# Attention of a hybrid encoder step: three engines in one written order, units in three lags, and prompt masks written by VectorE

## The chip, the cores and the metric

The kernel runs on one core of one Trainium2 chip. Its time is device microseconds from the start to the end of the program. The core has a matrix engine (TensorE, PE), three engines for elementwise work (VectorE or DVE, ScalarE or ACT, GpSimd or POOL), a sync engine (SP) that issues most transfers, and DMA queues. Each engine works through its own instructions one after another, and semaphores hold an instruction back until what it reads has been written and what it overwrites has been read.

## The reference

One inference step of an encoder with two layers, in float32, on 384 tokens: 256 frames of one prompt and 16 frames of each of 8 running sequences. Layer 0 mixes with a Mamba block, layer 1 with attention; behind each stands a PEER layer (a product-key mixture of 16384 experts). Only the attention is touched here. Cut to it:

```python
kv = rmsnorm(h, norm_kv) @ a_w_kv + a_b_kv            # 1024 -> 512: four heads of K and V, 64 wide
q = xn @ a_w_q[j] + a_b_q[j]                          # 1024 -> 1024: 16 heads, four to each K/V head
# prompt: a frame sees the keys of its own chunk of 64 and of the two chunks before it
probs = sink_softmax(jnp.where(valid, scores, -jnp.inf), sinks)   # the sink is one more logit, without a value
# sequence: the 128 cached keys and the 16 new ones
mix = o @ a_w_o[j] + a_b_o[j]
h = h + mix
h = h + peer(rmsnorm(h, norm_ffn[l]), ...)
```

## The kernel before, in words

The program is mamba, peer, attention, peer. Tokens lie in three blocks of 128: blocks 0 and 1 are the prompt, block 2 the eight sequences. Every large product is made exact enough by splitting both operands: a weight tile `raw` (128x1024) arrives by a DMA of SP (L152), ACT casts it to `hi` (L132), and DVE writes the rest to `lo` (L133). A product is then three matmuls: hi by hi, hi by lo, lo by hi. The helper `split` does it; `ring` gives the two `hi` and two `lo` buffers, a third where a pool for it is named (then `hix` and `lox`).

**Head.** The scaled rows of h are turned by PE (L897) and split into `khi`, `klo` and `qhi`, `qlo`; the K/V projection accumulates over eight row tiles in `accs` (L183). Then come query tiles 0 and 1 (`q_tile`: 24 matmuls at L168 to L170, ACT adds the bias into `qT` at L936, DVE copies the sequences' part to `qs` at L939), and K is turned to `kT` (L954, L956).

**Units.** 16 units of work follow, in the list `todo`. A prompt unit (p) is one block of queries and one K/V head: block 0 has 128 keys (called p0 below), block 1 has 256 (p1). A sequence unit (s) is two sequences and two K/V heads, 256 keys. The order is p0, p1, p0, p1, s, s, s, s, and that again, with two K/V heads to each half. A unit passes through these steps:

- scores: PE lays a mask (a matmul of a bf16 mask by the identity `idb`, L978) into the unit's PSUM banks and adds the score products (L988 or L998). A p unit has two banks, an s unit one.
- DVE takes the largest score (L1005, one reduction to a bank) and from it the negative offset `nm` (L1006) and the sink's exponent `es` (L1007).
- ACT takes the exponents to `sm`, two to a bank, each with its row sum in `den` (L1014), and that of `es` (L1008).
- DVE makes the shares: sum, reciprocal, and `sm` scaled (L1017, L1018, L1021).
- PE turns `sm` (L1031); ACT copies the first bank of a p unit to `pT` (L1037), DVE the other bank and that of an s unit (L1035).
- PE takes the products with the values (L1049 or L1062), ACT copies them to `oT` (L1051, L1066).

**Order.** In the loop (L1089 to L1106) a turn i writes the scores of unit i, the transposes of unit i-2 and the values of unit i-3. `pin` keeps PE's matmuls in the order in which they are written. For DVE and ACT nothing is fixed: the tile scheduler orders their instructions. Six query tiles (`q_at`) and four output terms (the last four turns) lie between the units. An output term is one 128-row tile of w_o against the split `oT` (`ohi`, `olo`): 12 matmuls for the two prompt blocks, 6 for the third block.

**Tail.** After the loop come the third block's first four terms (their weights loaded a second time), then terms 4, 5 and the pair 6 and 7 for all blocks. The adds of the result to h (`add`, L1122), the squares for the norm (L205) and the first projection (L1227) belong to the second call of `peer`. So does the load of its first weight tile `p_w_q`, which ACT casts to `hix`.

The masks come from POOL, which fills three bf16 tiles (L866 to L874) before it issues the seven loads of constants (L849 to L856).

Of the kernel before, what the change touches and what calls it, by code (L numbers as in the profile page):

```python
# [19 lines left out]
P = 128  # L20
# [48 lines left out]
def encoder_step(ctx: ExitStack, tc: tile.TileContext, t_in, t_out):  # L69
# [759 lines left out]
    def attention():  # L829
        with ExitStack() as c:  # L830
# [30 lines left out]
            mask0 = T(one, [P, 2, P], BF16, tag="mask0")  # L861
            mask1 = T(one, [P, 2, NP], BF16, tag="mask1")
            maskS = T(one, [P, NSEQ, NP], BF16, tag="maskS")

            def masked():
                pool.memset(mask0, 0.0)  # L866
                pool.memset(mask0[0:64, :, 64:128], NEG)
                pool.memset(mask1, 0.0)
                pool.memset(mask1[0:64, :, 192:256], NEG)
                pool.memset(mask1[64:128, :, 0:64], NEG)  # L870
# [18 lines left out]
            kw = {0: load_raw(t_in["w_kv"][0:P, :], 512)}  # L889
            turned = {}  # L890
# [8 lines left out]
            with in_order():  # L899
# [3 lines left out]
                hi0 = ring(512, F32R, "hi", 2)  # L903
                lo0 = ring(512, F32R, "lo", 2)
                act.copy(hi0, kw[0])
# [3 lines left out]
                dve.tensor_tensor(lo0, kw[0], hi0.bitcast(F32), op=OP.subtract)  # L909
                nrm.scale(1, xn[:, 1], 2)  # L910
                for b, n in ((2, 3), (0, 2), (1, 1)):
# [3 lines left out]
                accs = [[bank([P, 512])] for _ in range(NB)]  # L915
                for k in range(KD):
# [9 lines left out]
                split(qhi[:, KD - 1], qlo[:, KD - 1], turned[KD - 1], scale=gcol[:, 1, KD - 1:KD])  # L926
                dve.tensor_copy(idb, ident)
            with tc.issue_after(nrm.last.ins):
                masked()
                constants()  # L930
            kctx.__exit__(None, None, None)

            def q_tile(ct):
                ps = bank([P, NT])
                gemm_cols(ps, load_split(t_in["w_q"][ct]), qhi, qlo, 0, NT)
                act.activation(qT[:, ct], ps, AF.Identity, bias=bq[:, ct:ct + 1])  # L936
                n, g2 = divmod(ct, 2)
                for half in range(2):
                    dve.tensor_copy(qs[:, :, n, 2 * g2 + half],  # L939
                                    qT[64 * half:64 * half + 64, ct, NP:].rearrange("p (s t) -> p s t", t=TS))  # L940

            q_tile(0)
            q_tile(1)
            for b in range(NB):
                dve.tensor_tensor(kv[:, b], accs[b][0], bkv, op=OP.add)
            dve.tensor_scalar(nsnk, snk, -1.0, None, op0=OP.mult)
            dve.tensor_scalar(nsnks, snks, -1.0, None, op0=OP.mult)


            for n in range(4):  # L950
                ps = bank([P, NT])
                for r2 in range(2):
                    for b in range(NB):
                        pe.matmul(ps[64 * r2:64 * r2 + 64, b * P:(b + 1) * P], kv[:, b, n * 64:(n + 1) * 64], ident,  # L954
                                  start=True, stop=True)
                act.copy(kT[:, n], ps)  # L956
# [8 lines left out]
            P_, PT, SC = {}, {}, {}  # L965
            LAG = 2
# [970 lines left out]
```

## Time and profile before

| | us |
|---|---|
| median of three runs | 2348.94 |
| lowest and highest | 2347.12, 2353.32 |
| profiled execution: its own time | 2349.98 |
| its span, first to last instruction | 2348.3 |
| PE busy | 2299.7 (98%) |
| DVE busy | 1979.3 (84%) |
| ACT busy | 1246.7 (53%) |
| mean granted TensorE clock | 0.995 |

The attention takes from 1282.67 us (the first transposes) to 1436.0 us (the first transposes of the second peer); the loop's first mask is at 1321.10. The page's shares are an average over four stages with different limits, so what the change does is read from windows of these 153 us. In the timeline a row is start, duration, engine, line, operation, tiles, shape, count, and in brackets the idle time before it with the instruction that ended it.

### The profile page before, as it was taken

The numbers are of one execution on the slowest core, as the hardware profiler recorded it, in microseconds if no ns is written. First come the engines' busy times: TensorE is split into PE (matmuls) and PEld (weight loads), VectorE is DVE, ScalarE is ACT, GpSimd is POOL, SyncE is SP. The second block draws the span as 40 slices with busy tenths as digits, with TensorE's granted clock in tenths as the row PEclk, the third lists the DMA queues.
The fourth block names the chain that finished last, engine by engine and source line by source line (L and its number), as shares of the span: only waits on it lengthen the run. The fifth ranks groups of instructions, "written<-read, shape, count | busy, mean of one in ns | idle before, by whom it ended". The sixth has DMA issues, their size and how long they took to land. (4 is left out here: it accounts for less than half of the span.)

```text
span 2348.3 us, 43951 instructions
## 1 busy us (share of the span) xinstructions
PE 2299.7 (98%) x16376; PEld 1965.5 (84%) x16377; DVE 1979.3 (84%) x4234; ACT 1246.7 (53%) x2388; POOL 764.7 (33%) x779
## 2 busy tenths in 40 slices
PE   7999999999999999999999999999999999999998
PEld 7889988999999997667776778999999997667775
DVE  5899955979998999888876676979998999888876
ACT  5555624334476676554444555334476666554443
POOL 2223300011154324555563100011154324555562
PEclk9999999999999999999999999999999999999999
DMA  5554445367699889999996515357699889999997
GB/s 187 194 195 168 160 156 170 118 211 255 232 362 340 313 305 330 384 371 390 409 419 268 166 64 173 124 204 255 233 362 342 314 304 334 382 368 394 406 419 283
DMA packets 177944, 649.74 MB, mean 277 GB/s; under 512 B 21233, under 2 KB 23137, under 8 KB 175329
## 3 DMA queue, kind: packets, MB, share of 16 engines
q1 hardware_dynamic: 100800, 365.85, 42.6%
q0 software_dynamic: 76928, 281.07, 31.9%
q8 instruction: 129, 2.11, 0.4%
q14 instruction: 87, 0.70, 0.1%
HBM read 630.62 MB, written 18.06 MB: 276 GB/s over the span
## 5 line engine op out<-in xcount | busy, mean ns | idle before, releaser
L132 ACT CAST hi<-raw 128x1024 fp32r<-128x1024 f32 (+1 forms) x439 | 457.8, 1043 | 615.8 <-PE bank L169 280.8
L133 DVE TENSOR_TENSOR lo<-raw,hi 128x1024 fp32r<-128x1024 f32 (+1 forms) x439 | 531.0, 1210 | 182.1 <-ACT hi L132 181.6
L1433 POOL DMA_INDIRECT gath<-in_p_u,eidU x226 | 289.4, 1281 | 825.3 <-DVE gath L1482 505.9
L168 PE MATMUL bank<-xhi,hi 128*128 128x256 f32 (+1 forms) x1184 | 344.8, 291 | 1.3 <-ACT hi L132 1.3
L170 PE MATMUL bank<-xhi,lo 128*128 128x256 f32 (+1 forms) x1184 | 338.9, 286 | 3.6 <-DVE lo L133 3.6
L169 PE MATMUL bank<-xlo,hi 128*128 128x256 f32 (+1 forms) x1184 | 338.0, 285 | 0.0
L1433 POOL DMA_INDIRECT G<-in_p_v,eidT x192 | 225.1, 1173 | 79.7 <-issue 53.0
L168 PEld LDWEIGHTS bank<-xhi,hi 128*128 128x128 f32 x1184 | 223.2, 189 | 11.3 <-issue 5.9
L168 PE MATMUL bank<-qhi,hi 128*128 128x256 f32 (+1 forms) x784 | 232.7, 297 | 0.0
L170 PE MATMUL bank<-qhi,lo 128*128 128x256 f32 (+1 forms) x784 | 227.1, 290 | 2.2 <-DVE lo L133 2.2
L169 PE MATMUL bank<-qlo,hi 128*128 128x256 f32 (+1 forms) x784 | 228.3, 291 | 0.0
L170 PEld LDWEIGHTS bank<-xhi,lo 128*128 128x128 f32 x1184 | 222.7, 188 | 6.5 <-DVE lo L133 6.0
L169 PEld LDWEIGHTS bank<-xlo,hi 128*128 128x128 f32 x1184 | 223.1, 188 | 0.8 <-issue 0.2
L1596 ACT ACTIVATE oa<-ioh,e2T 128x128 f16<-128x128 f16 x512 | 163.3, 390 | 94.3 <-PE bank L1608 94.3
L183 PE MATMUL bank<-hi,phi 128*128 128x512 f32 x632 | 206.1, 405 | 1.5 <-ACT phi L132 1.5
L132 ACT CAST hix<-raw 128x1024 fp32r<-128x1024 f32 x118 | 123.9, 1050 | 150.5 <-PE bank L183 72.6
L183 PE MATMUL bank<-lo,phi 128*128 128x512 f32 x632 | 197.7, 392 | 0.9 <-DVE lo L133 0.9
L183 PE MATMUL bank<-hi,plo 128*128 128x512 f32 x632 | 196.4, 390 | 0.0
L133 DVE TENSOR_TENSOR lox<-raw,hix 128x1024 fp32r<-128x1024 f32 x118 | 143.6, 1217 | 22.3 <-ACT hix L132 21.9
L183 PEld LDWEIGHTS bank<-hi,phi 128*128 128x128 f32 x632 | 113.6, 188 | 49.5 <-ACT phi L132 17.5
L170 PEld LDWEIGHTS bank<-qhi,lo 128*128 128x128 f32 x784 | 147.8, 189 | 2.6 <-DVE lo L133 2.6
L169 PEld LDWEIGHTS bank<-qlo,hi 128*128 128x128 f32 x784 | 148.8, 190 | 0.4
(397 smaller groups left out, 5357.3 us busy)
## 6 DMA issues: line engine op xcount, KB each, us to landing
raw<-in_u_t SPq DMA_DIRECT2D x256, 512.0 KB
raw<-in_p_v SPq DMA_DIRECT2D x256, 512.0 KB
raw<-in_w_in SPq DMA_DIRECT2D x32, 512.0 KB
raw<-in_p_w_q SPq DMA_DIRECT2D x32, 512.0 KB
raw<-in_w_z SPq DMA_DIRECT2D x16, 512.0 KB
s<-in_state_ssm SPq DMA_DIRECT2D x8, 1024.0 KB
out_sm_ssm<-s SPq DMA_DIRECT2D x8, 1024.0 KB
raw<-in_w_out SPq DMA_DIRECT2D x16, 512.0 KB
```

What stands on the lines that cost most here:

```text
L132: act.copy(hi, raw)
L133: dve.tensor_tensor(lo, raw, hi32, op=OP.subtract)
L168: pe.matmul(ps, whi[:, s], xhi[:, k, c0:c1], start=(k == 0), stop=False)
L169: pe.matmul(ps, whi[:, s], xlo[:, k, c0:c1], start=False, stop=False)
L170: pe.matmul(ps, wlo[:, s], xhi[:, k, c0:c1], start=False, stop=(k == KD - 1))
L183: mm = pe.matmul(halves[hf], x, w[:, hf * n:(hf + 1) * n], start=s_, stop=e_)
L1433: pool.indirect_dma_start(out=tile_, out_offset=None, in_=tab, in_offset=bass.IndirectOffsetOnAxis(ap=idx, axis=0))
L1596: act.activation(a[:, i], ioh, AF.Square, scale=-1.0, bias=e2T[:, t, 0:1])
```

## The change

Only the attention differs; the first peer and the mamba block keep the order of every engine. What the changed program does:

- **Written order.** `in_order` chains the instructions of PE, DVE and ACT, each in the order in which the program writes them, so that the scheduler doesn't move them. Before, it held the head up to the K/V projection; now it also holds query tiles 0 and 1, the turning of K, the whole loop and the output terms behind it.
- **Lags.** A turn writes: the eviction of a query tile, shares of unit i-1, transposes of unit i-2, scores of unit i, the first 16 matmuls of a query tile, the largest of unit i, its exponents, an output term, values of unit i-3, the last 8 matmuls of the query tile, the split of the next weight tile, and, in some turns, an add of the bias to h or a split of `oT`.
- **Weights.** Weight tiles are loaded two ahead (`load_ahead`) and split at named places (`step_weights`), one tile ahead of their use, with a third `hi` and `lo` in a pool of their own (`a5`).
- **Masks.** The 16 mask matmuls of the prompt units and the five POOL memsets of their masks go. Instead DVE writes NEG into the scored banks, 64 rows by 2x64 elements at a time: two memsets for a p0 unit, four for a p1 unit, 24 in all, ahead of each reduction. The s units keep their mask matmuls.
- **Output terms.** The third block's first four terms move from behind the loop to three added turns 16, 17 and 18, beside the shares, transposes and values of the last units.
- **Head.** The split for row tile k+1 of the K/V projection is written ahead of the matmuls of tile k; the masks and constants are issued ahead of query tile 0.

```diff
+            def load_ahead(n):
+                while stream_of and len(ahead_) < n:
+                    ahead_.append(load_raw(stream_of.pop(0)))
+
+            def step_weights():
+                load_ahead(2)
+                if ahead_:
+                    wts.append(split_raw(ahead_.pop(0)))
+                    load_ahead(2)
...
+                kv_part(0)
                 for k in range(KD):
-                    split(khi[:, k], klo[:, k], turned[k], scale=gcol[:, 4, k:k + 1])
-                    nxt = load_split(t_in["w_kv"][(k + 1) * P:(k + 2) * P, :], 512) if k < KD - 1 else None
                     if k:
-                        split(qhi[:, k - 1], qlo[:, k - 1], turned[k - 1], scale=gcol[:, 1, k - 1:k])
+                        q_part(k - 1)
+                    if k < KD - 1:
+                        nxt = load_split(t_in["w_kv"][(k + 1) * P:(k + 2) * P, :], 512)
+                        kv_part(k + 1)
+                    else:
+                        q_part(k)
+                        step_weights()
...
+            def largest(u):
...
                 for q, ps in enumerate(pss):
+                    if kind == "p":
+                        dve.memset(ps[0:64, :, nk - 64:nk], NEG)
+                        if i:
+                            dve.memset(ps[64:128, :, 0:64], NEG)
                     dve.tensor_reduce(nm[:, q], ps, axis=AX.X, op=OP.max)
...
+            N = len(todo)
             q_at = {0: 2, 1: 3, 3: 4, 5: 5, 7: 6, 8: 7}
+            o_at = {N - 4: [0], N - 3: [1], N - 2: [2], N - 1: [3], N: [0, 1], N + 1: [2], N + 2: [3]}
...
+            extra = c.enter_context(tc.tile_pool(name="a5", bufs=1))
+            more.update(hi=(extra, 1), lo=(extra, 1))
...
+            with in_order():
+                for i in range(N + 3):
+                    q_evict()
+                    if 0 <= i - 1 < N:
+                        shares(todo[i - 1])
+                    if 0 <= i - 2 < N:
+                        transposes(todo[i - 2])
+                    if i < N:
+                        scores(todo[i])
+                    if i in q_at:
+                        tile_ = q_tile(q_at[i])
+                        next(tile_)
+                    if i < N:
+                        largest(todo[i])
...
+                    if i < N:
+                        exps(todo[i])
+                    for ct in o_at.get(i, ())[:1]:
+                        lo_ = i >= N
+                        gemm_rows(accs[2:] if lo_ else accs[:2], [out_term(ct, 2 * lo_)], ct == 0, False)
+                        step_weights()
+                    if 0 <= i - 3 < N:
+                        values(todo[i - 3])
+                    for ct in o_at.get(i, ())[1:]:
+                        gemm_rows(accs[2:], [out_term(ct, 2)], False, False)
+                        step_weights()
+                    if i in q_at:
+                        next(tile_)
+                        step_weights()
+                    if i in (5, 6, 7):
+                        dve.tensor_tensor(h[:, i - 5], h[:, i - 5], bo, op=OP.add)
+                    if N - 5 <= i < N - 1:
+                        out_split(i - (N - 5))
+                    elif N - 1 <= i < N + 1:
+                        for ct in (4, 5) if i == N - 1 else (6, 7):
+                            out_split(ct, 0, NP)
+                for ct in range(4, 8):
+                    out_split(ct, NP, NT)
+                step_weights()
+                for ct in (4, 5):
+                    gemm_rows(accs, [out_term(ct)], False, False)
+                    step_weights()
+                gemm_rows(accs, [out_term(6), out_term(7)], False, True)
+                more.clear()
```

The first place where it shows is DVE in turns 2 and 3, where units 2 (a p0 unit) and 3 (a p1 unit) follow each other. Before, the reductions of both units (`nm_15208` and `nm_15250`) stand ahead of the shares of either (`den_15210`, `den_15252`):

```order
L1005 TENSOR_REDUCE nm_15208<-bank_15191 128x2 [waits PE_49]
L1035 COPY pT_15244<-bank_15239 128x512 [waits PE_49]
L1006 SCALAR_TENSOR_TENSOR nm_15208<-nm_15208,nsnk_14666 128x4 [waits DVE_49]
L1005 TENSOR_REDUCE nm_15250<-bank_15228 128x2 [waits PE_49]
L1006 SCALAR_TENSOR_TENSOR nm_15250<-nm_15250,nsnk_14666 128x4 [waits DVE_49]
L1017 TENSOR_TENSOR den_15210<-den_15210,es_15209 128x4 [waits Activation_49]
L1021 TENSOR_SCALAR sm_15219<-sm_15219,den_15210 128x128 x2
L1017 TENSOR_TENSOR den_15252<-den_15252,es_15251 128x4 [waits Activation_49]
```

In the change (unit 2 has `den_15216`, unit 3 `nm_15273` and `den_15275`):

```order
L1065 TENSOR_TENSOR den_15216<-den_15216,es_15215 128x4 [waits Activation_49]
L1069 TENSOR_SCALAR sm_15226<-sm_15226,den_15216 128x128 x2
L1084 COPY pT_15248<-bank_15243 128x512 [waits PE_49]
L1041 MEMSET bank_15250 64x2x64 [waits PE_49]
L1043 MEMSET bank_15250 64x2x64 [waits DVE_49]
L1044 TENSOR_REDUCE nm_15273<-bank_15250 128x2 [waits DVE_49]
L1044 TENSOR_REDUCE nm_15273<-bank_15251 128x2 [waits DVE_49]
L1045 SCALAR_TENSOR_TENSOR nm_15273<-nm_15273,nsnk_14666 128x4 [waits DVE_49]
L133 TENSOR_TENSOR lo_15306<-raw_15123,hi_15305 128x1024 [waits DMAHW6_49,Activation_49]
L963 COPY qs_14684<-qT_14682 64x8x16 [waits Activation_49]
L1065 TENSOR_TENSOR den_15275<-den_15275,es_15274 128x4
L1069 TENSOR_SCALAR sm_15287<-sm_15287,den_15275 128x256 x2
```

Unit 3's reduction now stands behind the whole of unit 2's shares and a `pT` copy; behind it come the rest of a weight tile and the query copy, and only then unit 3's own shares.

The second is ACT at the same place. Before, the exponents of units 2 and 3 (`nm_15208`, `nm_15250`) stand next to each other with one `oT` copy between:

```order
L1014 ACTIVATE sm_15219,den_15210<-bank_15191,nm_15208 128x128
L1051 COPY oT_14680<-bank_15270 128x2x128 [waits PE_49]
L1014 ACTIVATE sm_15258,den_15252<-bank_15228,nm_15250 128x256 [waits DVE_49]
L1014 ACTIVATE sm_15261,den_15252<-bank_15229,nm_15250 128x256
L132 CAST hi_15529<-raw_15527 128x1024 [waits DMAHW7_49,PE_49,Activation_49]
```

In the change the exponents of unit 3 wait for the `nm_15273` of the rows above, and the cast of a weight tile, of which `lo_15306` is the rest, stands behind them:

```order
L1059 ACTIVATE es_15215<-es_15215 128x4 [waits DVE_49]
L1086 COPY pT_15241<-bank_15236 128x512 [waits PE_49]
L1056 ACTIVATE sm_15284,den_15275<-bank_15250,nm_15273 128x256 [waits DVE_49,PE_49]
L1056 ACTIVATE sm_15287,den_15275<-bank_15251,nm_15273 128x256
L1101 COPY oT_14678<-bank_15291 128x2x128 [waits PE_49]
L132 CAST hi_15305<-raw_15123 128x1024 [waits DMAHW6_49,Activation_49]
L960 ACTIVATE qT_14682<-bank_15256,bq_14663 128x384 [waits PE_49]
```

So a turn with a weight tile runs exponents, `oT` copy and cast on ACT, then the rest of the tile on DVE, then the shares.

The third is ACT at the end of the attention: the cast of the second peer's first weight tile, then the squares of h (L205). Before:

```order
L132 CAST hi_16255<-raw_16253 128x1024 [waits DMAHW6_49,DVE_49,PE_49]
L132 CAST hix_16341<-raw_16333 128x1024 [waits DMAHW7_49]
L205 ACTIVATE qTp_16324,ss_2852_16338<-h_14514 128x512 [waits DVE_49] x5
```

In the change:

```order
L132 CAST hi_16267<-raw_16225 128x1024 [waits DMAHW4_49,DVE_49,PE_49]
L132 CAST hix_16354<-raw_16346 128x1024 [waits DMAHW5_49,DVE_49,PE_49]
L205 ACTIVATE qTp_16337,ss_2850_16351<-h_14514 128x512 [waits DVE_49] x5
```

The cast has gained waits for DVE and PE: its buffer lies where pool `a5` held a third `hi` of the attention, which the last output terms still read. On DVE its `lox` stands ahead of all six adds to h, as before.

More of the change, by code (lines that the diff above doesn't have):

```diff
@@ L942, in attention, with q_tile @@
[L942 to L956, printed above, removed]
+                def q_tile(ct):
+                    whi, wlo = wts.pop(0)
+                    ps = bank([P, NT])
+                    for k in range(KD):
+                        w = whi[:, k * P:(k + 1) * P]
+                        pe.matmul(ps, w, qhi[:, k], start=(k == 0), stop=False)
+                        pe.matmul(ps, w, qlo[:, k], start=False, stop=False)
+                    yield
+                    for k in range(KD):
+                        pe.matmul(ps, wlo[:, k * P:(k + 1) * P], qhi[:, k], start=False, stop=(k == KD - 1))
+                    q_out.append((ct, ps))
+                    yield
@@ new lines, in q_evict, with k_turn @@
+                def q_evict():
+                    while q_out:
+                        ct, ps = q_out.pop(0)
+                        act.activation(qT[:, ct], ps, AF.Identity, bias=bq[:, ct:ct + 1])
+                        n, g2 = divmod(ct, 2)
+                        for half in range(2):
+                            dve.tensor_copy(qs[:, :, n, 2 * g2 + half],
+                                            qT[64 * half:64 * half + 64, ct, NP:].rearrange("p (s t) -> p s t", t=TS))
+                def k_turn(n):
+                    ps = bank([P, NT])
+                    for r2 in range(2):
+                        for b in range(NB):
+                            pe.matmul(ps[64 * r2:64 * r2 + 64, b * P:(b + 1) * P], kv[:, b, n * 64:(n + 1) * 64], ident,
+                                      start=True, stop=True)
+                    return ps
@@ new lines, in attention @@
+                with tc.issue_after(nrm.last.ins):
+                    masked()
+                    constants()
+                q_out = []
+                for _ in q_tile(0):
+                    pass
+                for b in range(NB):
+                    dve.tensor_tensor(kv[:, b], accs[b][0], bkv, op=OP.add)
+                step_weights()
+                dve.tensor_copy(idb, ident)
+                dve.tensor_scalar(nsnk, snk, -1.0, None, op0=OP.mult)
+                dve.tensor_scalar(nsnks, snks, -1.0, None, op0=OP.mult)
@@ L957, in attention @@
+                q_evict()
+                pk = k_turn(0)
+                act.copy(kT[:, 0], pk)
+                for _ in q_tile(1):
+                    pass
+                step_weights()
+                q_evict()
+                for n in range(1, 4):
+                    pk = k_turn(n)
+                    act.copy(kT[:, n], pk)
+            kctx.__exit__(None, None, None)
             pool.dma_start(t_out["pr_k"], kv[:, 1, 0:256])
@@ L962, in attention, with scores @@
                                    kv[s * TS:(s + 1) * TS, 2, i * 256:(i + 1) * 256])
[L965 to L968 removed]
+            SM, PT, live = {}, {}, {}
+            def scores(u):
                 kind, i, n = u
                 if kind == "p":
[L972 to L983 removed]
                     nk = (P, NP)[i]
+                    pss = [bank([P, 2, nk]) for _ in range(2)]
                     for j in range(2):
@@ L992, in scores @@
                     nk = NP
+                    pss = [bank([P, 2, NP])]
+                    pe.matmul(pss[0], idb, maskS[:, 2 * i:2 * i + 2], start=True, stop=False)
                     for s in range(2):
@@ L1088, in attention @@
-            first = len(todo) - 4
-            for i in range(len(todo) + LAG + 1):
-                if i in (5, 6, 7):
-                    pin(dve.tensor_tensor(h[:, i - 5], h[:, i - 5], bo, op=OP.add))
-                if i < len(todo):
-                    masks(todo[i])
-                if 0 <= i - LAG < len(todo):
-                    transposes(todo[i - LAG])
-                if i < len(todo):
-                    scores(todo[i])
-                if 0 <= i - LAG - 1 < len(todo):
-                    values(todo[i - LAG - 1])
-                if i in q_at:
-                    q_tile(q_at[i])
-                if i == first - 1:
-                    accs += [[bank([P, 512]) for _ in range(2)] for _ in range(2)]
-                if 0 <= i - first < 4:
-                    ct = i - first
-                    out_split(ct)
-                    gemm_rows(accs, [out_term(ct)], ct == 0, False)
@@ L1109, in attention, with out_split @@
[L1109 to L1118 removed]
+            def out_split(ct, c0=0, c1=NT):
+                split(ohi[:, ct, c0:c1], olo[:, ct, c0:c1], oT[:, ct, c0:c1])
```

105 lines of the change are left out of this document (42 added, 63 removed).

## The prediction

> **What bounds the kernel now.** I first read the attention by windows: the head, the loop with its tail, the start of the second peer up to its first projection, and eight microseconds inside the tail. Columns: window, length, busy time and instructions of PE, its weight loads, DVE, ACT and POOL, then the granted clock and DMA.
>
> ```profile
> 1282.67:1321.10 38.43, 35.58 (x209) 28.20 (x207) 24.13 (x42) 20.00 (x37) 18.30 (x42) 1.00 0.69 213
> 1321.10:1436.00 114.90, 108.85 (x936) 89.42 (x937) 77.48 (x203) 60.25 (x187) 0.62 (x2) 0.97 0.29 95
> 1436.00:1440.03 4.03, 2.54 (x19) 1.85 (x18) 2.54 (x7) 2.57 (x7) 1.03 (x2) 1.00 0.57 234
> 1406.00:1414.00 8.00, 8.00 (x79) 6.91 (x78) 2.86 (x6) 3.45 (x9) 0.00 (x0) 0.57 0.28 89
> ```
>
> PE sets the loop: 108.85 of 114.90 us. DVE and ACT have room as a sum, which says nothing yet of how their steps hang together. The last row shows a granted clock of 0.57 for 8 us, so 8 x 0.43 = 3.4 us of clock are lost. Next come the waits of PE in the whole attention (total, count, longest):
>
> ```profile
> PE bank L1031 <- DVE sm L1021: 2.8, 2, 1.5
> PE bank L988 <- ACT qT L936: 1.6, 1, 1.6
> PE bank L183 <- DVE lo L133: 0.9, 2, 0.8
> PE bank L897 <- DVE xlo L136: 0.8, 1, 0.8
> ```
>
> All that PE waits here is 6.1 us; the windows allow 6.05 of idle time in the loop and 2.85 in the head. More than that no better order can win, beside the clock and removed work.
>
> What the scheduler's order does for PE stands in the timeline of DVE around units 2 (p0) and 3 (p1); `nm` is what the exponents wait for, `den` starts the shares:
>
> ```profile
> 1337.37 0.74 DVE L1005 TENSOR_REDUCE nm<-bank 128x2 f32<-128x256 f32 x2
> 1338.74 0.16 DVE L1006 SCALAR_TENSOR_TENSOR nm<-nm,nsnk 128x4 f32<-128x4 f32 x1
> 1339.02 1.28 DVE L1005 TENSOR_REDUCE nm<-bank 128x2 f32<-128x512 f32 x2
> 1340.33 0.16 DVE L1006 SCALAR_TENSOR_TENSOR nm<-nm,nsnk 128x4 f32<-128x4 f32 x1
> 1340.57 0.16 DVE L1017 TENSOR_TENSOR den<-den,es 128x4 f32<-128x4 f32 x1
> 1340.98 0.88 DVE L1021 TENSOR_SCALAR sm<-sm,den 128x128 f32<-128x128 f32 x4
> 1342.76 0.16 DVE L1017 TENSOR_TENSOR den<-den,es 128x4 f32<-128x4 f32 x1 [0.90 <-ACT sm L1014]
> 1343.17 1.14 DVE L1021 TENSOR_SCALAR sm<-sm,den 128x256 f32<-128x256 f32 x4
> ```
>
> and in that of ACT:
>
> ```profile
> 1338.94 0.37 ACT L1014 ACTIVATE sm<-bank,nm 128x128 f32<-128x128 f32 x1 [1.35 <-DVE nm L1006]
> 1340.67 0.50 ACT L1014 ACTIVATE sm<-bank,nm 128x256 f32<-128x256 f32 x1
> 1342.48 0.24 ACT L1014 ACTIVATION_READ_ACCUMULATOR sm<-bank,nm 128x1 f32 x1
> 1393.02 0.47 ACT L1014 ACTIVATE sm<-bank,nm 128x256 f32<-128x256 f32 x1 [1.09 <-DVE nm L1006]
> 1393.93 0.20 ACT L1008 ACTIVATE es<-es 128x2 f32<-128x2 f32 x1
> ```
>
> DVE reduces unit 3 (1339.02) while ACT takes the exponents of unit 2 (from 1338.94), and makes unit 2's shares (1340.57) while ACT is at unit 3 (from 1340.67). The two engines overlap across units.
>
> **The change, part by part.** Write L for the largest of a unit with its memsets up to `nm`, E for its exponents, S for its shares. In the written order, DVE does S(i-1), the `pT` copy of unit i-2, L(i), [rest of a weight tile, query copy]; ACT does E(i), `oT` copy, [cast of the weight tile]. E(i) waits for L(i), which stands behind S(i-1), which waits for E(i-1). So L, E and S run one after another, unit by unit: while ACT is at E(i), DVE has nothing that it may do. The cast stands behind E(i), and the rest of the tile, which waits for it, ahead of S(i): both lie in the chain as well, in each turn that splits a weight tile. That is the added wait of this change. Behind it queue on DVE the shares, the next reductions, and with them PE's transposes.
>
> Prices by group (count, then busy and mean ns):
>
> ```profile
> L133 DVE TENSOR_TENSOR lo<-raw,hi 128x1024 fp32r<-128x1024 f32 x11 | 13.4, 1217 | 3.8 <-ACT hi L132 3.8
> L1005 DVE TENSOR_REDUCE nm<-bank 128x2 f32<-128x512 f32 x16 | 10.7, 682 | 0.4 <-PE bank L998 0.3
> L1035 DVE COPY pT<-bank 128x512 f32<-128x512 f32 x11 | 7.6, 687 | 5.2 <-PE bank L1031 5.2
> L939 DVE COPY qs<-qT 64x128 f32<-64x128 f32 x14 | 3.0, 216 | 0.1
> L1035 DVE COPY pT<-bank 128x256 f32<-128x256 f32 x4 | 1.7, 415 | 0.0
> L132 ACT CAST hi<-raw 128x1024 fp32r<-128x1024 f32 x10 | 10.4, 1048 | 7.9 <-issue 2.8 <-PE bank L169 2.8 <-PE bank L183 1.1
> L1051 ACT COPY oT<-bank 128x256 f32<-128x256 f32 x8 | 3.0, 373 | 7.8 <-PE bank L1049 7.8
> ```
>
> A DVE memset in a bank is not in the trace. Bounds from rows: 0.16 us (`nm`, 128x4) below, 0.41 (the reduction of 128x256, 3.1 us by 8) above, were it to cost what reading a bank costs; with 64x128 elements the query copy, 0.216, is nearest, so 0.2. All 24 are then 4.8 us (3.8 to 9.9), and nothing covers them, since ACT waits for the reduction behind them.
>
> L: p0 0.74 + 0.2 + 2 x 0.2 = 1.35; p1 1.28 + 0.2 + 4 x 0.2 = 2.3; s 0.68 + 0.2 = 0.9. E: p0 1.5 (four rows about 0.38 apart from 1338.94 on), p1 1340.67 to 1342.72 less the sink's exponent, 1.9; s 1393.02 to 1394.0, 1.0. S: p0 1340.57 to 1341.8, 1.25; p1 1342.76 to 1344.3, 1.55; s, with two scalings in place of four, 1.0. A weight tile: 0.35 (`oT`) + 1.05 + 1.2 = 2.6; its query copy 0.45.
>
> | turns | S(i-1) + pT + L + E | further | sum |
> |---|---|---|---|
> | 0 (p0), with scores and the first exponent's table | 5.2 | 2.7 | 7.9 |
> | 1 (p1) | 1.25 + 0 + 2.3 + 1.9 | 2.7 | 8.2 |
> | 2 (p0) | 1.55 + 0.4 + 1.35 + 1.5 | | 4.8 |
> | 3 (p1) | 1.25 + 0.7 + 2.3 + 1.9 | 3.05 | 9.2 |
> | 4 (s) | 1.55 + 0.4 + 0.9 + 1.0 | | 3.85 |
> | 5 and 7 (s), each with an add of bo to h, 1.2 | 1.0 + 0.7 + 0.9 + 1.0 | 4.25 | 15.7 |
> | 6 (s), its add under E | 3.6 | | 3.6 |
> | 8 (p0) | 1.0 + 0.7 + 1.35 + 1.5 | 3.05 | 7.6 |
> | 9 (p1) | 1.25 + 0.7 + 2.3 + 1.9 | | 6.15 |
> | 10 (p0) | 1.55 + 0.4 + 1.35 + 1.5 | | 4.8 |
> | 11 (p1), a split of `oT`, 1.05 | 1.25 + 0.7 + 2.3 + 1.9 | 1.4 | 7.55 |
> | 12 to 15 (s), each a w_o tile | 3.6, the first 3.85 | 2.7 | 25.5 |
>
> The sum is 104.85: in the change the shares of the last unit start 105 us into the loop, unless PE is later. Before they start here:
>
> ```profile
> 1405.28 0.61 DVE L1021 TENSOR_SCALAR sm<-sm,den 128x256 f32<-128x256 f32 x2
> ```
>
> that is 84.2 us in. The chain is 21 us longer than what PE now needs, so PE gets stalls in its place, above all where a p1 unit or a weight tile comes (turns 2, 3, 5, 7, 10 to 12): spread over five to seven places, 3 to 4 us each. The loads of weights, two tiles ahead on SP, don't count: the loop's DMA share is 0.29.
>
> **Tail.** From there on 30.7 us passed before (1405.28 to 1436.0). Of it the third block's first four terms, 24 matmuls of 128x512 at 0.227 from start to start, 5.4 us, move beside the last units; the 1.3 us stall and the waits for `lo` go, weight tiles being ready. What is left: turns 16 to 18 (S, transposes, values, the moved terms beside them, the splits) 8.2 and terms 4 to 7, 72 x 0.227 = 16.4, together 24.6. Loop and tail: 105 + 24.6 = 129.6 against 114.9, **+14.7**. The mask matmuls that PE saves lie in that already; with PE waiting they buy nothing.
>
> **Head.** Splits one tile ahead, and constants earlier for want of five POOL memsets; PE can win at most its idle 2.85 and the least is 0: -2.5, as the two splits that it waits for both move.
>
> **Clock.** The drop at 1406 came after one 1.3 us stall and the small value products. Five longer stalls leave room for more such drops. A drop cost 3.4 us, part of which lies where PE waits anyway: +4, bounds 0 and 9 (nearly three at full price).
>
> **Start of the peer.** Here is the end before:
>
> ```profile
> 1435.77 0.39 PE L183 MATMUL bank<-hi,olo 128*128 128x512 f32 x1
> 1427.18 1.04 ACT L132 CAST hix<-raw 128x1024 fp32r<-128x1024 f32 x1
> 1429.59 0.68 DVE L1122 TENSOR_TENSOR h<-h,bank 128x512 f32<-128x512 f32 x1
> 1432.12 0.69 DVE L1122 TENSOR_TENSOR h<-h,bank 128x512 f32<-128x512 f32 x1 [0.68 <-PE bank L183]
> 1434.23 1.30 DVE L1122 TENSOR_TENSOR h<-h,bank 128x512 f32<-128x512 f32 x2
> 1436.20 0.69 DVE L1122 TENSOR_TENSOR h<-h,bank 128x512 f32<-128x512 f32 x1 [0.34 <-PE bank L183]
> 1440.03 0.44 PE L1227 MATMUL bank<-qhi,hix 128*128 128x384 f32 x1
> ```
>
> Five of six adds were done beside the last matmuls; the sixth starts 0.2 after the end, the projection 3.83 after that. In the change the cast to `hix` waits for readers of the third `hi`, about 0.6 us before the end X. It ends at X+0.45, `lox` at X+1.65, and all six adds and all squares queue behind. Three adds at 0.65 apart, from the third to the fourth 2.1 (a norm step lies between, as from 1432.12 to 1434.23), one more, a norm step's start: the sixth starts at 1.65 + 2 x 0.65 + 2.1 + 0.65 + 0.8 = X+6.5, the projection at X+10.3 against 4.03: **+6.3**. If the wait is met early it is 0; if the norm steps don't overlap at all, 9.5.
>
> Sum: 14.7 - 2.5 + 4 + 6.3 = +22.5. The profiled execution took 2349.98, 1.0 above the median; the change comes to 2372.5 on its scale, **2371** on that of the median 2348.94.
>
> Against this change speaks a rule of the Trainium skill, "TensorE: Matmul & The Clock Gate", section "HAM oscillation — how this bites in real kernels": "no PE-idle gaps >~3.4µs", or the clock falls to half and must be earned back. By it the 1.3 us stall should have cost nothing, and the row of 0.57 shows a loss; so this trace has the clock fall more easily, and the rule alone would be too mild.
>
> **Rivals.**
>
> - **Faster: the written order closes PE's gaps.** PE's 6.1 us of waits, the 3.4 of clock and the 15 to 16 prompt masks go. The masks cost:
>
> ```profile
> L978 PE MATMUL bank<-mask,idb 128*128 128x512 bf16 x7 | 2.2, 386 | 0.0
> L978 PE MATMUL bank<-mask,idb 128*128 128x256 bf16 x8 | 1.6, 278 | 0.0
> ```
>
>   at most 3.8. Together 13.3: 2336. It decides from the point where the chain is no longer than PE's 84 us: the ten weight tiles, 26 us of it, would have to run beside it. For it: DVE is idle during each E. Against it: the rest of a tile waits for a cast that stands behind that same E.
> - **Loop longer, edges free.** The chain holds but the clock doesn't fall and the cast to `hix` finds its buffer free: 14.7 - 2.5 = +12.2, 2361. For it: stalls of a few us come between dense runs of query matmuls. Against it: the wait on PE is written into that cast.
> - **The clock falls at each long stall.** Five stalls at 3.4 are 17 in place of 4: +35, less what is hidden behind waits, some 5: 2379. The rule quoted above would have it so for stalls over its bound.
> - **No change.** Half of the chain's surplus is hidden by steps that I set too long and the head wins all it can: +21 becomes about 10, tail -6, head -2.8, the peer's start a few us: 2352.
>
> **How the numbers follow.** Forecast 0.60, longer loop alone 0.15, clock 0.10, no change 0.09, faster 0.06. A measurement of this kernel tells 0.3%, 7 us, from no change: slower 0.85, same 0.09, faster 0.06. The range takes the low bounds (memsets at 0.16, no clock loss, the peer's start at half, together -8) and the high ones (memsets at 0.41, +5; clock 9, +5; the peer's start +3): 2363 to 2384 by these, and to 2356 and 2386 for the neighbouring cases, which leaves out most of the two cases of no loss.
>
> **What would show it.** Right: the shares of the last unit start near 105 us into the loop; exponents of unit i+1 never begin before the shares of unit i have ended; PE waits for `sm` and `qT` by 15 us or more; `hix` starts under a microsecond before the attention's last matmul and the projection some 10 us after it; further windows with a clock under 0.8. Wrong: PE over 95% busy in the loop; the adds to h beside the last matmuls; memset rows above 0.4 or missing.

## The result and the profile after

| | before | changed |
|---|---|---|
| median | 2348.94 (2344.98 to 2353.32, five runs) | 2379.36 (2376.2 to 2380.74, five runs) |
| ratio, with its 95% interval | | 1.0122 (1.0106 to 1.0139) |
| span of the profiled execution | 2348.3 | 2378.1 |

The change is 30 us slower. The forecast was 2371, with 2356 to 2386 as its range. One execution in all those below, of the kernel with pinned adds, took 4508.16 us in the slow state and is left out of that kernel's ratio. Where the 29.8 us between the two spans lie, by the stages of the prediction:

| stage | before | changed | difference | forecast |
|---|---|---|---|---|
| up to the first transposes | 1282.67 | 1283.39 | +0.7 | 0 |
| head, to the first scores | 38.75 | 37.78 | -1.0 | -2.5 |
| loop, to the scaling of the last unit's shares | 83.86 | 111.06 | +27.2 | +21 and a part of the clock's +4 |
| tail, to the end of the last output matmul | 30.88 | 25.67 | -5.2 | -6.1 |
| from there to the peer's first projection | 3.87 | 10.81 | +6.9 | +6.3 |
| rest | 908.27 | 909.39 | +1.1 | 0 |

The first scores are at 1321.42 us before, 0.3 behind the first mask, from which the forecast counted head and loop; the change has no mask there. By the forecast's mark the head shrinks by 0.6 and the loop grows by 26.9.

The windows of the changed kernel, for the same three stages, then turn 5 (columns as before):

```profile
1283.39:1321.17 37.78, 34.32 (x208) 28.71 (x206) 24.86 (x43) 19.45 (x36) 16.20 (x37) 1.00 0.70 216
1321.17:1457.90 136.73, 116.26 (x921) 93.75 (x920) 79.50 (x220) 56.25 (x182) 0.00 (x0) 0.89 0.22 71
1457.90:1468.71 10.81, 3.97 (x20) 3.55 (x19) 8.01 (x16) 6.03 (x16) 1.65 (x3) 0.66 0.50 195
1353.10:1363.00 9.90, 9.90 (x49) 8.61 (x49) 4.35 (x15) 2.97 (x12) 0.00 (x0) 0.53 0.12 47
```

In the loop PE is idle for 136.73 - 116.26 = 20.5 us, before 6.05. DVE has 2 us more work than before and ACT 4 us less (79.5 and 56.25 us, against 77.48 and 60.25), and both have far more time for it: by these sums no engine is the bound, which leaves the order; the experiments try it. PE's waits in the attention and at the peer's start:

```profile
PE bank L1080 <- DVE sm L1069: 11.2, 5, 4.2
PE bank L1251 <- issue: 5.5, 1, 5.5
PE bank L183 <- ACT ohi L132: 4.2, 1, 4.2
PE bank L1016 <- ACT qT L960: 3.8, 1, 3.8
PE bank L183 <- ACT xhi L135: 1.7, 2, 1.5
```

Five waits for shares (`sm`), one for the split of `oT`, one for `qT`: 19.2 us in the loop. The timeline of turn 3 (unit 3, a p1 unit) shows how one of them comes about, DVE first:

```profile
1347.06 0.16 DVE L1045 SCALAR_TENSOR_TENSOR nm<-nm,nsnk 128x4 f32<-128x4 f32 x1
1350.58 1.22 DVE L133 TENSOR_TENSOR lo<-raw,hi 128x1024 fp32r<-128x1024 f32 x1 [3.16 <-ACT hi L132]
1351.73 0.45 DVE L963 COPY qs<-qT 64x128 f32<-64x128 f32 x2
1352.18 0.16 DVE L1065 TENSOR_TENSOR den<-den,es 128x4 f32<-128x4 f32 x1
1352.60 1.14 DVE L1069 TENSOR_SCALAR sm<-sm,den 128x256 f32<-128x256 f32 x4
```

then ACT:

```profile
1347.32 0.47 ACT L1056 ACTIVATE sm<-bank,nm 128x256 f32<-128x256 f32 x1 [4.15 <-DVE nm L1045]
1349.22 0.38 ACT L1101 COPY oT<-bank 128x256 f32<-128x256 f32 x1
1349.48 1.08 ACT L132 CAST hi<-raw 128x1024 fp32r<-128x1024 f32 x1
1354.96 0.47 ACT L1056 ACTIVATE sm<-bank,nm 128x256 f32<-128x256 f32 x1 [3.66 <-DVE nm L1045]
```

and PE:

```profile
1353.10 1.94 PE L1080 MATMUL bank<-ident,sm 128*128 128x128 f32 x8 [3.02 <-DVE sm L1069]
1357.78 0.52 PE L950 MATMUL bank<-xlo,hi 128*128 128x384 f32 x1
```

The chain runs as it was written down: exponents from 1347.32, the `oT` copy, the cast, then the rest of the tile at 1350.58, the query copy, and only at 1352.18 the shares, whose operands had been there since 1349.4. ACT is idle for 4.15 and 3.66 us, DVE for 3.16, and each waits for the other. PE, which waited 3.02, then runs at half clock: a matmul of a query tile, 0.33 to 0.35 long at full clock, takes 0.52.

The memsets of a p1 unit later in that loop:

```profile
1400.06 0.17 DVE L1041 MEMSET bank<- 64x128 f32 x1
1400.33 0.17 DVE L1043 MEMSET bank<- 64x128 f32 x1
1400.53 0.69 DVE L1044 TENSOR_REDUCE nm<-bank 128x2 f32<-128x512 f32 x1
1402.50 0.16 DVE L1045 SCALAR_TENSOR_TENSOR nm<-nm,nsnk 128x4 f32<-128x4 f32 x1
```

One takes 0.17, but each of them and each reduction waits for the one before on the same bank. From the first memset to `nm` it is 2.44 us; two reductions to `nm` took 1.31 before (1339.02 to 1340.33). Four memsets cost 1.13, 0.28 each.

The start of the peer, ACT, DVE and PE of the changed kernel:

```profile
1457.51 0.39 PE L183 MATMUL bank<-hi,olo 128*128 128x512 f32 x1
1457.26 1.05 ACT L132 CAST hix<-raw 128x1024 fp32r<-128x1024 f32 x1 [10.51 <-PE bank L183]
1458.34 1.23 DVE L133 TENSOR_TENSOR lox<-raw,hix 128x1024 fp32r<-128x1024 f32 x1
1459.48 1.88 DVE L1191 TENSOR_TENSOR h<-h,bank 128x512 f32<-128x512 f32 x3
1464.62 0.68 DVE L1191 TENSOR_TENSOR h<-h,bank 128x512 f32<-128x512 f32 x1
1468.71 0.67 PE L1296 MATMUL bank<-qhi,hix 128*128 128x384 f32 x1
```

ACT stands 10.51 us at the cast, until 0.6 us before the last matmul ends (1457.90). The six adds come behind it, the last at 1464.62, 6.7 us after that end, where the forecast had 6.5.

### The profile page after: what moved, and what is told of

Read it like the earlier page. It is cut to its first block, busy times and chain, and to the rows that moved or that the text cites. A ratio compares the mean times of both kernels' runs of the same rounds, so it can differ in the third digit from the quotient of the medians.

```text
span 2378.1 us, 43966 instructions
## 1 busy us (share of the span) xinstructions
PE 2307.7 (97%) x16361; PEld 1973.2 (83%) x16361; DVE 1988.1 (84%) x4262; ACT 1245.2 (52%) x2392; POOL 769.4 (32%) x774
## 4 chain that ended last, share of the span: by engine, by line
PE 86%; DVE 7%; ACT 3%; DMA 2%; issue 2%; another core or an unknown queue 0%; POOL 0%; SPq 0%; POOLq 0%; DVEq 0%; ACTq 0%
PE bank L183 30%; PE bank L168 11%; PE bank L170 11%; PE bank L169 10%; PE bank L1622 4%; PE bank L1710 4%; PE bank L1635 2%; PE bank L1677 2%; PE bank L703 2%; PE bank L724 2%; PE bank L704 2%; DVE lo L133 2%; ACT hi L132 1%; ACT sm L1056 1%; DMA gath<-in_p_u,eidU 0%
## 5 line engine op out<-in xcount | busy, mean ns | idle before, releaser
L132 ACT CAST hi<-raw 128x1024 fp32r<-128x1024 f32 (+1 forms) x434 | 452.4, 1042 | 591.5 <-PE bank L169 264.5
L133 DVE TENSOR_TENSOR lo<-raw,hi 128x1024 fp32r<-128x1024 f32 (+1 forms) x434 | 524.9, 1210 | 194.4 <-ACT hi L132 174.8
L168 PE MATMUL bank<-xhi,hi 128*128 128x256 f32 (+1 forms) x1120 | 323.4, 289 | 1.2 <-ACT hi L132 1.2
L170 PE MATMUL bank<-xhi,lo 128*128 128x256 f32 (+1 forms) x1120 | 318.4, 284 | 4.5 <-DVE lo L133 3.9
L169 PE MATMUL bank<-xlo,hi 128*128 128x256 f32 (+1 forms) x1120 | 316.9, 283 | 0.0
L168 PEld LDWEIGHTS bank<-xhi,hi 128*128 128x128 f32 x1120 | 211.5, 189 | 10.3 <-issue 5.2
L170 PEld LDWEIGHTS bank<-xhi,lo 128*128 128x128 f32 x1120 | 211.1, 188 | 7.9 <-DVE lo L133 6.5
L132 ACT CAST hix<-raw 128x1024 fp32r<-128x1024 f32 x124 | 130.1, 1050 | 163.4 <-PE bank L183 74.1
L169 PEld LDWEIGHTS bank<-xlo,hi 128*128 128x128 f32 x1120 | 211.5, 189 | 0.4
L133 DVE TENSOR_TENSOR lox<-raw,hix 128x1024 fp32r<-128x1024 f32 x124 | 151.2, 1219 | 33.9 <-ACT hix L132 32.5
```

What stands on the lines that cost most here:

```text
L132: act.copy(hi, raw)
L133: dve.tensor_tensor(lo, raw, hi32, op=OP.subtract)
L168: pe.matmul(ps, whi[:, s], xhi[:, k, c0:c1], start=(k == 0), stop=False)
L169: pe.matmul(ps, whi[:, s], xlo[:, k, c0:c1], start=False, stop=False)
L170: pe.matmul(ps, wlo[:, s], xhi[:, k, c0:c1], start=False, stop=(k == KD - 1))
```

## The experiments

The kernels were timed in groups, each beside runs of the kernel before, whose median was 2348.94 beside the change and 2348.19 (the first four below), 2351.84 (the next three) and 2350.08 (the last three). So times are compared by their ratios, and one profiled execution of each kernel shows where time went: "head", "loop" and "peer" are the stages above, loop and tail in one.

| | median | ratio to before (95%) | head | loop | peer |
|---|---|---|---|---|---|
| before | 2348.94 | | 38.75 | 114.74 | 3.87 |
| the change | 2379.36 | 1.0122 (1.0106 to 1.0139) | 37.78 | 136.73 | 10.81 |
| third buffer turned | 2368.16 | 1.0085 (1.0068 to 1.0102) | 38.02 | 135.38 | 3.87 |
| no memsets | 2367.30 | 1.0087 (1.0070 to 1.0104) | 36.81 | 124.93 | 10.80 |
| PE alone in order | 2355.17 | 1.0032 (1.0018 to 1.0046) | 42.69 | 110.27 | 10.81 |
| early weights | 2362.78 | 1.0066 (1.0049 to 1.0083) | 38.11 | 122.61 | 10.81 |
| gaps filled | 2377.48 | 1.0118 (1.0098 to 1.0137) | 38.26 | 132.82 | 10.81 |
| written order, four moves | 2354.36 | 1.0012 (0.9999 to 1.0024) | 38.59 | 118.28 | 3.87 |
| PE alone, buffer, adds pinned | 2355.98 | 1.0012 (1.0002 to 1.0023) | 39.04 | 119.06 | 3.93 |
| the same, adds anchored | 2347.96 | 0.9989 (0.9980 to 0.9998) | 38.53 | 111.89 | 3.94 |
| the same, masks by PE | 2346.52 | 0.9976 (0.9965 to 0.9986) | 39.41 | 108.87 | 3.93 |
| four moves, masks by PE | 2346.76 | 0.9986 (0.9977 to 0.9995) | 39.42 | 110.30 | 3.87 |

The theory is the prediction's: a chain of largest, exponents, weight tile and shares bounds the loop, and the blocked cast delays the peer. The rivals are the clock, and the other parts of the change.

**The third buffer turned by one place.**

```diff
-            turn_of.update(hi=1, lo=1)
+            turn_of.update(hi=2, lo=2)
```

> The change with the ring of weight buffers turned by one place, so that the third buffer holds w_o tile 5 in place of tile 6 at the end; nothing else. Chain theory with a late start of the peer: the cast for the second peer's first weight tile no longer waits for the attention's last matmuls (it starts some 8 us earlier), the adds to h lie beside them again, and the first projection starts about 4 us after the attention in place of 10.8: 2379.4 - 6 to - 7 = about 2373. Rival, that the peer's late start is only the rest of the loop's delay (adds and squares slow of themselves): within 1.5 us of 2379.

The cast to `hix` starts 8 us before the last matmul ends:

```profile
1447.82 1.05 ACT L132 CAST hix<-raw 128x1024 fp32r<-128x1024 f32 x1 [3.02 <-PE bank L183]
1455.55 0.39 PE L183 MATMUL bank<-hi,olo 128*128 128x512 f32 x1
1459.81 0.44 PE L1296 MATMUL bank<-qhi,hix 128*128 128x384 f32 x1
```

The stage is back at 3.87, its length before the change: 6.9 us, and the blocked buffer is shown to be the cause. The time fell by 0.37% of the kernel, 8.7 us by the ratios, somewhat more than that stage and than the 6 to 7 expected; 1.4 of the rest lie in the loop.

**No memsets.** The prompt's scores are not masked in this kernel.

```diff
-                    if kind == "p":
-                        dve.memset(ps[0:64, :, nk - 64:nk], NEG)
-                        if i:
-                            dve.memset(ps[64:128, :, 0:64], NEG)
```

> The change without its 24 memsets: the prompt units' scores are not masked at all, so this leaves the prompt mask out. Chain theory: each memset lies on the serial chain, 0.25 us from start to start by the rows of the changed kernel, 6 us in all: 2373 to 2375, the shares of the last unit 5 to 6 us earlier than 111 us into the loop. Rival, that PE and the clock set the loop: within 2 us of 2379.

The loop is 11.8 us shorter, twice what was expected. By the rows above the memsets cost 4 x 1.13 and 4 x 0.52 (p0: 1.30 in place of 0.78), 6.6 us. A further 3.7 is turn 5, 7.6 us here and 11.3 in the change: its query tile no longer runs at half clock. The rival, that PE and the clock set the loop, has fallen. Of the remaining 1.5 us, 0.9 lie in the turns of the eight prompt units and 0.6 in turn 12. By the ratios the time falls by 8.2 us, which is above the 4 to 6 expected too.

**PE alone in the written order.**

```diff
-            with in_order():
+            with in_order((mybir.EngineType.PE,)):
                 for i in range(N + 3):
```

> The change with only PE held in the written order in the loop and behind it; DVE and ACT are ordered by the scheduler as they were before. Memsets, lags, the early weights and the moved output terms stay. Chain theory: the loss in the loop comes from the written order of DVE and ACT, so most of it goes: 2358 to 2366, with the reductions of the next unit ahead of the shares again. Rival, that the lags, the memsets or the moved terms make the loss: above 2374.

The loop falls to 110.27 us, 26.5 below the change and 4.5 below the kernel before, with the same lags, memsets, moved terms and weight tiles split one ahead. The median, 2355, lies below the expected range. Unit 3 is reduced ahead of unit 2's shares again, on DVE:

```profile
1341.44 1.27 DVE L1044 TENSOR_REDUCE nm<-bank 128x2 f32<-128x512 f32 x2
1342.82 0.15 DVE L1065 TENSOR_TENSOR den<-den,es 128x4 f32<-128x4 f32 x1
```

So the written order of DVE and ACT makes the loss in the loop; the rival that the lags, the memsets or the moved terms make it has fallen, since all of them stay here. The scheduler moved the three adds of bo to h, 3.5 us of DVE, out of this loop into the head, which is 4.9 longer: PE waits 2.63 us behind them, and the clock is at 0.50 there for 3.4 us (1302.1 to 1305.6), which can cost 1.7 more at most.

```profile
1305.78 3.50 DVE L1174 TENSOR_TENSOR h<-h,bo 128x1024 f32<-128x1024 f32 x3 [0.50 <-DMA bo<-in_b_o]
1309.87 0.50 PE L183 MATMUL bank<-hi,xlo 128*128 128x512 f32 x1 [2.63 <-DVE xlo L136]
```

**Early weights.** The split of the next tile is written between the largest and the exponents, so that the cast fills ACT's wait for `nm` and the rest of the tile DVE's wait for the exponents.

```diff
+                    if i in q_at or N - 4 <= i < N:
+                        step_weights()
                     if i < N:
                         exps(todo[i])
...
                         next(tile_)
-                        step_weights()
```

> The change with the split of the next weight tile written between the largest of a unit and its exponents, in the turns 0 to 15: the cast then stands ahead of the exponents on ACT, the rest of the tile beside them on DVE. Chain theory: ten tiles at 2.25 us leave the chain, of which part was hidden or becomes PE's work: 12 to 20 us less, 2359 to 2367. Rival, that the clock or the one-by-one run of largest, exponents and shares alone sets the loop: 2374 or more.

16.6 us less by the medians, 13.2 by the ratios, both inside the range; the loop is 14.1 shorter. In written order, too, about half of the 30 us goes with one step moved. Turn 5 went from 11.3 to 5.7; as the filled gaps below show, 3.7 of that is its half clock, which went with the wait.

**Gaps filled.** Throwaway matmuls ahead of PE's waits keep it busy.

```diff
+                    if warm[0] and q == 0:
+                        for _ in range(warm[0] * 2 // nkb):
+                            pe.matmul(pt.rearrange("p n k q -> p (n k q)"), idb, ..., start=True, stop=True)
...
+                    warm[0] = {2: 14, 3: 4, 5: 11, 7: 2, 10: 7, 11: 16}.get(i, 0)
...
+                        if i == N - 4:
+                            for _ in range(16):
+                                pe.matmul(accs[0][0], idb, ..., start=True, stop=True)
```

> The change with throwaway bf16 mask matmuls put where PE waits in the loop: 2 to 16 of 128x512 ahead of the transposes of turns 2, 3, 5, 7, 10 and 11 and ahead of the first output term in turn 12, into banks that are overwritten; 70 matmuls of about 0.22 us. They replace waiting, so they add work but no result. Clock theory: without those gaps the clock stays at 1.00 in the loop, the query tile of turn 5 no longer runs at half speed, the shares of the last unit come at 106 to 108 in place of 111 us, and the time falls by 3 to 6: 2373 to 2376. Rival, that the half clock only lies where PE waits anyway: within 2 us of 2379, or 2 to 4 slower by the added matmuls.

The same 14 us around turn 5, of the change and then of this kernel:

```profile
1350.00:1364.00 14.00, 10.98 (x55) 9.47 (x54) 6.77 (x21) 4.96 (x17) 0.00 (x0) 0.63 0.11 39
```

```profile
1350.00:1364.00 14.00, 11.38 (x100) 8.94 (x100) 10.29 (x30) 5.05 (x17) 0.00 (x0) 1.00 0.22 74
```

With the gap filled the clock stays at 1.00 in this window. The loop is 3.9 us shorter (132.82), the last shares at 107.1, as the clock theory had it. Turn 5 alone falls from 11.3 to 7.6. The medians (2377.5, ratio 1.0118 against 1.0122) can't tell 4 us apart. So the clock's share in the loop is about 4 us, not more: three of the four half-clock stretches go, and only one of them cost anything that PE didn't wait for anyway.

**Written order with four moves.** Early weights; the adds of bo and the splits of `oT` beside them; the query copy of DVE behind the shares; the buffer turned.

```diff
                     if i in q_at or N - 4 <= i < N:
                         step_weights()
+                    if i in (5, 6, 7):
+                        dve.tensor_tensor(h[:, i - 5], h[:, i - 5], bo, op=OP.add)
+                    if N - 5 <= i < N - 1:
+                        out_split(i - (N - 5))
...
                         shares(todo[i - 1])
+                    q_copy()
```

> The change, still in one written order of three engines, with four moves: weight tiles split between the largest and the exponents; the adds of bo to h and the splits of oT written at the same place; the query copies of DVE behind the shares; the third weight buffer holding w_o tile 5 at the end. Chain theory: 16.6 us by the early weights and 11.2 by the buffer, as measured alone, and further 1.0 to 1.2 in each of some eight turns, half of it hidden: 2379.4 - 28 - 5 = 2346, with 2342 to 2352. Rival, that largest, exponents and shares one by one bound it from there on: 2352 or more.

The median, 2354, is beyond the expected range; its ratio, 1.0012, puts it at the edge between the range and the rival (2352 beside the 2349 of the first group). It is 25 to 26 us less than the change where 33 were expected. The loop is 18.4 shorter, of which the early weights alone had given 14.1, and the peer's start 6.9. So the further moves gave 4.3, near the 5 expected; most of the error lay in the sum, which was made of two differences of medians (16.6 and 11.2) of which the stages show 14.1 and 8.3. Which of the further moves gave how much was not tried.

**PE alone in order, buffer turned, adds pinned.** `pin` around the adds, as before the change.

> The change with PE alone held in the written order in the loop, the adds of bo to h kept at their place as before the change, and the third weight buffer holding w_o tile 5 at the end. The run with PE alone in order lost 4.6 us in the head, where the scheduler had put those adds, and 6.9 at the peer's start. Chain theory: 2355.2 - 4.6 - 6.9 = 2343.7, that is 4 to 6 below the kernel before, the loop's 110 us in place of 114.7 being the gain of the moved terms and masks. Rival, that the gain in that loop belongs to the adds put early: 2347 or more.

Missed: the ratio is 1.0012 where 0.998 was expected, some 8 us. The head is repaired (39.0), the peer too, but the loop is at 119.06. `pin` keeps the adds in order among themselves only, as the rows show: written in turns 5 and 6, two of them went into turns 2 and 3, on DVE ahead of unit 2's reduction and ahead of the shares of units 2 and 3:

```profile
1337.01 1.22 DVE L1174 TENSOR_TENSOR h<-h,bo 128x1024 f32<-128x1024 f32 x1
1345.03 1.23 DVE L133 TENSOR_TENSOR lo<-raw,hi 128x1024 fp32r<-128x1024 f32 x1 [2.35 <-PE bank L953]
1346.18 1.22 DVE L1174 TENSOR_TENSOR h<-h,bo 128x1024 f32<-128x1024 f32 x1
1347.31 0.23 DVE L1065 TENSOR_TENSOR den<-den,es 128x4 f32<-128x4 f32 x2
```

From unit 1's shares to unit 3's it took 13.2 us, in place of 9.4 with PE alone in order. Not all of this is the adds' own time: the scheduler put the rest of a weight tile ahead of the shares as well, and the loop has 17 us at half clock, against 3.4 there.

**The same, adds anchored.** Each add is held behind the `nm` of its turn.

```diff
-                        pin(dve.tensor_tensor(h[:, i - 5], h[:, i - 5], bo, op=OP.add))
+                        with tc.issue_after(last_nm[0].ins):
+                            dve.tensor_tensor(h[:, i - 5], h[:, i - 5], bo, op=OP.add)
```

> As the run with PE alone in order and the third buffer holding w_o tile 5, but each add of bo to h held behind the nm of its turn (5, 6, 7) and not placed by the scheduler. Theory: of 2356, the loop's 119 us go back to about 111, as where no add lies in it; head 38.5, peer's start 3.9: about 3.5 us below the kernel before, ratio 0.998 to 0.999. Rival, that the loop of 110 us was won by having the adds in the head: loop 113 or more, ratio 1.000 or above.

As expected: loop 111.89, ratio 0.9989. So the places of three adds of 1.2 us, with what the scheduler moved along and the clock (6.8 us at half), made 7 us of the loop. The moved terms, the weight tiles split one ahead and the lags, with DVE and ACT left to the scheduler and the memsets' cost included, are worth about 3 us of the loop together; they were not tried one by one.

**Masks by PE again**, in this kernel and in the one with four moves.

```diff
+                    for ps in pss:
+                        pe.matmul(ps, idb, (mask0, mask1)[i], start=True, stop=False)
...
-                        dve.memset(ps[0:64, :, nk - 64:nk], NEG)
```

> As the run with the anchored adds, with the prompt masks made by PE again (16 mask matmuls, five POOL memsets, no memset on DVE). Theory: where the scheduler overlaps DVE and ACT, 24 memsets at 0.28 (6.7 us of DVE) and 3 us of PE are near to each other in price: within 3 us of the anchored run. Rival, that DVE's memsets cost their full price there too: loop 3 to 6 us shorter.

> The written order of three engines with the four moves (2354, loop 118 us), and the prompt masks made by PE again. Chain theory: the memsets leave the chain, 6.6 us, and PE gets 3 us of work where it waits 5 to 10 us: the loop at 112 to 114 us, ratio 0.997 to 0.999. Rival, that PE sets this loop by now: within 2 us of 118, ratio 1.001 or above.

The loops shrink by 3.0 us (2.7 from the first mask on), at the border of what the two theories expected, and by 8.0, more than the 4 to 6 expected. The loop windows of the two:

```profile
1321.38:1430.25 108.87, 106.29 (x937) 86.48 (x937) 75.47 (x203) 59.32 (x190) 0.79 (x2) 1.00 0.28 98
```

```profile
1323.72:1434.02 110.30, 107.08 (x937) 86.26 (x937) 79.37 (x205) 60.52 (x192) 0.78 (x2) 1.00 0.28 99
```

PE is busy for 98 and 97% of them, at full clock. The memsets, put on DVE to spare PE 3 us, cost more than they spare in either order, and most where the order is written. Part of both gains is the clock: the loops with memsets have two stretches at half clock each, 6.8 us with the adds anchored and 10.2 with the four moves, those with masks by PE none; how much these stretches cost was not tried. For the scheduler's order the intervals of the two ratios overlap a little, so there the gain rests on the windows. Both kernels beat the one before, the first by 0.24% (0.14 to 0.35%), some 5.6 us, the second by 0.14% (0.05 to 0.23%). In the second all three engines are in one written order, so that order is not slow of itself; which rows it puts where decides.

## Why the prediction was right, and where it was off

- **The bound.** Right. PE's 6 us of waits were all there was to win, and the change made 20 of them.
- **The chain of L, E, S and the weight tile.** Right in kind: shares of unit i wait for the tile that waits for the exponents, as the rows of turn 3 show, and a loop without the written order of DVE and ACT lost all of its delay. Turn by turn the table holds within 0.6 us, with turn 5 as the one exception (11.3 against 7.85). At the end it stood at 104.85 and the shares at 110.7 us by the same mark (`den`): 3.4 of the 5.8 missing are turn 5, the half clock, and the rest are 0.1 to 0.6 in most turns, the p units above all. The +21 of the forecast compared two marks: 104.85 counts to the last `den`, 84.2 to the scaling of `sm`, which stood 2.2 behind `den` (1403.08) before and 0.4 in the change. From `den` to `den` the forecast was +22.9 and the measured +28.7; loop and tail together don't depend on it.
- **A memset.** Mis-sized: 0.2 in the table, 0.28 in the chain (24: 6.6 us, against 4.8). The row of one is 0.17; what was left out is that in written order a memset and the reduction behind it wait for each other on one bank. With PE alone in order the scheduler sets two memsets of different banks back to back, in 0.30 or 0.31 us. It lay within the bounds of 0.16 and 0.41.
- **The clock, +4.** The size was right (3.9, by the filled gaps), in part by luck: that four falls would come and only that of turn 5 cost anything was not worked out. The rival with a fall at each long stall was right on how often it falls, four times in the loop, and at the peer's start once more, and its time of 2379 was the one measured; but its price, 12 us of unhidden loss, was not: gaps filled gave back 4.
- **The tail.** -5.2 against -6.1. The last turns and the last four terms took 25.7 in place of 24.6: the first moved terms waited for their weights (0.25 and 0.53 us for `hix` and `lox`, 0.41 for `lo`).
- **The head.** Mis-sized: -1.0 (-0.6 by the forecast's own mark) against -2.5. A split written a tile ahead waits a tile earlier for its weights. ACT stood 3.49 us at the cast of a w_kv tile that was still on its way, and PE waited 1.46 for what stood behind that cast:

```profile
1301.34 0.62 ACT L132 CAST hi<-raw 128x512 fp32r<-128x512 f32 x1 [3.49 <-DMA raw<-in_w_kv]
1302.49 0.50 PE L183 MATMUL bank<-hi,xhi 128*128 128x512 f32 x1 [1.46 <-ACT xhi L135]
```

- **The peer's start, +6.3.** Right: +6.9, all of it gone with the buffer turned.
- **The sum.** +22.5 against 29.8. Of the 7.3 missing, 3.3 lie in loop and tail (22.0, against 14.7 + 4 with the clock), 1.5 in the head, 0.6 at the peer's start, and 1.8 before and behind these stages. The last stay unexplained; other runs differ there by as much.

## What to carry to other kernels

An order written by hand has to be read as a chain across engines: what a row waits for on the other engine, and what stands behind the row while it waits. Put work that depends on nothing, such as the split of a weight tile, into the place where its engine waits, not behind the work that the next step needs; that alone was worth 14 of 22 us of the loop here, 3.7 of them by the clock. When a pool lends a buffer to two stages, look which of its users ends last, since a cast at the head of the next stage will wait for it with all that is queued behind.

## What the runs showed of the hardware

The granted clock falls to 0.5 in stretches of 3.4, 6.8 or 10.2 us. Here are the edges of one of 10.2 us in the changed kernel, in windows of a quarter microsecond (the granted clock is the last number but two):

```profile
1351.75:1352.00 0.25, 0.00 (x0) 0.00 (x0) 0.24 (x3) 0.00 (x0) 0.00 (x0) 1.00 0.00 0
1352.00:1352.25 0.25, 0.00 (x0) 0.00 (x0) 0.24 (x2) 0.00 (x0) 0.00 (x0) 0.88 0.00 0
1352.25:1352.50 0.25, 0.00 (x0) 0.00 (x0) 0.22 (x2) 0.00 (x0) 0.00 (x0) 0.50 0.00 0
1362.00:1362.25 0.25, 0.25 (x2) 0.25 (x1) 0.00 (x0) 0.00 (x0) 0.00 (x0) 0.50 0.00 0
1362.25:1362.50 0.25, 0.25 (x2) 0.02 (x1) 0.00 (x0) 0.00 (x0) 0.00 (x0) 0.64 0.00 0
1362.50:1362.75 0.25, 0.25 (x3) 0.14 (x4) 0.00 (x0) 0.00 (x0) 0.00 (x0) 1.00 0.00 0
```

In the changed kernel's loop they run from 1335.1 to 1342.0, 1393.1 to 1400.0 and 1403.4 to 1410.2, and in the kernel before from 1406.5 to 1413.4: 6.8 us each, and the one of 10.2 (1352.2 to 1362.4). Other kernels have stretches of 3.4 us too, such as 1333.2 to 1336.6 without memsets. Those of the changed kernel's loop begin 2.1 to 3.5 us after PE went idle, in waits of 3.0 to 4.2 us; waits of 1.5, 1.6 and 2.04 us brought none in the kernels before and changed, but one of 1.30 us between small products did, before the change, and one of 2.32 us in the kernel with filled gaps. The Trainium skill, "TensorE: Matmul & The Clock Gate", section "HAM oscillation — how this bites in real kernels", puts the bound at idle gaps of about 3.4 us; waits of 3.02, 2.32 and 1.30 us were enough here.

The length of the wait does not decide it alone. The same wait of PE, behind the same matmuls, stands in two kernels, first with PE alone in order and then with the adds anchored:

```profile
1337.13 0.49 PE L1016 MATMUL bank<-kT,qT 64*128 64x128 f32 x4 [2.05 <-ACT qT L960]
```

```profile
1339.13 0.49 PE L1017 MATMUL bank<-kT,qT 64*128 64x128 f32 x4 [2.05 <-ACT qT L960]
```

In the first the clock stayed at 1.00 (1338 to 1344), in the second it was at 0.50 from 1340.3 to 1343.7. What else decides it was not tried. A stretch costs half of its length at most, 3.4 us for 6.8, and nothing where PE waits for its operands in that time.
